# A shared first modulation: ten blocks on the tensor engine in 128-column passes, six on VectorE, none on GpSimd

## The chip, the cores and the metric

The kernel runs on one core of a Trainium2 chip. The metric is the device time of one execution in microseconds. The engines are called as the profile calls them: PE (TensorE, matrix products; its weight loads are listed apart as PEld), DVE (VectorE), ACT (ScalarE), POOL (GpSimd), and SP (SyncE, which issues the fetches).

## The reference

A trunk of two layers works on 512 latent and 256 context tokens of width 1024. Each layer first makes six vectors of 1024 numbers (a shift, a scale and a gate for each of its two halves) from a condition vector, once for the latent tokens (`c`) and once for the context (`c_ctx`). Then it normalises the tokens, scales and shifts them, and projects them. Only this beginning of layer 0 is touched by the change:

```python
silu_c = jax.nn.silu(c)
silu_cc = jax.nn.silu(c_ctx)
for l in range(DEPTH):                                   # 2 layers
    mod = silu_c @ w_mod[l] + b_mod[l]                   # (1024) @ (1024, 6144)
    mod_c = silu_cc @ w_mod[l] + b_mod[l]
    sh1, sc1, g1, sh2, sc2, g2 = jnp.split(mod[:, None, :], 6, axis=-1)
    csh1, csc1, cg1, csh2, csc2, cg2 = jnp.split(mod_c, 6)
    h = rms_norm(x, norm1[l]) * (1 + sc1) + sh1          # 512 latent tokens
    hc = rms_norm(ctx, norm1[l]) * (1 + csc1) + csh1     # 256 context tokens
    ... = jnp.split(h @ w_in[l], IN_SPLITS, axis=-1)     # and hc @ w_in[l]
    ...  # neighbourhood and grouped-query attention, gated merge, residual, SwiGLU FFN
```

All arithmetic is in float32.

## The kernel before

**Layout.** Tokens lie along the free dimension, latent tokens in columns 0 to 511 and context tokens in 512 to 767. Channels lie along the 128 partitions, so the width of 1024 is eight channel blocks `k`. Each large product is made of three float32r passes: a number is split in a high part (`h`, `wh`, copied on ACT) and the rest (`hl`, `wl`, a subtraction), and high by high, high by rest and rest by high are added in PSUM. A weight block is 128x1024 (512 KB).

**The front.** `Trunk.start` is the first stage. It fetches the eight token blocks (`x`, 384 KB each, latent and context together), squares and adds them up (`square`, L573; `total`, L576), takes the means on PE (`means`, L581), adds epsilon (`eps`, L586), takes the power -1/2 on POOL (`power`, L591), spreads the result over the partitions on PE (`widen`, L597), and multiplies each token block by it (`normed`, L603).

Meanwhile it makes the first sixteen of the layer's 48 modulation blocks, of 128 channels each: blocks 0 to 7 are the shifts of the channel blocks 0 to 7, and 8 to 15 their scales. Channel block `k` so needs modulation blocks `k` and `k + 8`. A block is made in one of three ways:

- `p`: on PE (`product`, L611), with the weight block as the loaded operand and the two condition columns (latent and context) as a moving operand of 2 columns, over eight steps; the result stands in PSUM (`mp`);
- `d`: on DVE, two reductions (`reduced`, L616) of the transposed weight block with a condition row spread over the partitions (`crow`), one for each condition;
- `g`: one reduction on DVE for the latent condition, and for the context condition a product on POOL (`times`, L620) that ACT adds up along the row (`summed`, L623).

`settle` (L628 and L631) adds the bias on DVE, and for a scale also multiplies by the norm's gain. When a channel block has its shift and its scale, `modulate` scales and shifts it in place, on ACT (L638) or DVE (L640), once for the latent and once for the context columns. `high` copies the high part on ACT (L644), `low` subtracts on POOL or DVE (L648).

At last `multiply` (L673) does the first three projection blocks (`gk0`, `gv0`, `gq0`): for the 512 latent columns three passes for each channel block and projection block, and after all of these the same for the 256 context columns. Their weights are split by `whigh` (ACT, L659) and `wlow` (POOL or DVE, L663). Two rules of the plan fix their order: channel blocks `k` in rising order within a projection block, and the context columns of a projection block behind its latent ones.

**The order.** The string `FIRST` gives the order of the fetches and how each modulation block is made (`x` is a token block, `w` a projection weight). `HOWU`, `HOWL` and `HOWW` name the engine of `modulate`, `low` and `wlow` for each block (a is ACT, v DVE, g POOL). From these `start` makes a list of operations, each with an engine, a cost, what it waits for, and an urgency. `Ops.run` is a list planner: it gives each engine a clock, takes the operation that can begin first (at a tie, the more urgent one), and writes the instructions in the order of these planned beginnings. That order is then fixed for each engine. Fetches are planned, and issued by SP, in the order of `FIRST`. A fetch of a modulation block waits until an earlier block of the same buffers has been used up, which the plan writes as `free[-5]`. Where PE has a gap in the plan, `run` fills it to 80% with small products of the identity (`idle`, L725, 0.215 us each in the plan).

The planned costs that matter here are `PROD` for a product on PE, 1.14 us for a reduction, and those of `low` (0.87 on DVE, 1.76 on POOL) and `wlow` (1.13 and 2.31).

**What follows.** Behind the front stand the rest of layer 0's projections and its attention, in an order written from a plan of their own, then the merge, the output projection and the FFN, and layer 1. The remaining modulation blocks are made beside these on DVE. The front's small pool has five row buffers of 128x1024 (two for `crow`, three `junk`) and five weight buffers; the tiles `x`, squares, `h` and `hl` come from a common store of 45 slots of 128x768.

Of the kernel before, what the change touches and what calls it, by code (L numbers as in the profile page):

```python
# [13 lines left out]
F32R = mybir.dt.float32r  # L14
AF = mybir.ActivationFunctionType
ALU = mybir.AluOpType
# [4 lines left out]
P = 128  # L21
D = 1024
KB = D // P
# [21 lines left out]
for _n in ORDER:  # L45
    for _j in range(COLS[_n][1]):
# [28 lines left out]
]  # L75


FIRST = "x x x x 10p x x x x 0g 8d 1g 13p w 9p w 2p 11g 12p 3d w 4g 5g 6g 14d 7d 15g"

HOWU, HOWL, HOWW = "aaavaaav", "ggvggvgv", "ggv"  # L80
START, HOP, LAND = 4.06, 0.15, 0.25
SAME = dict(v=0.22, a=0.0, g=0.0, p=0.0)
WARM = 0.8
PROD = 2.5


RATE = dict(a=(0.06, 0.00083, "a"), e=(0.28, 0.00083, "a"), v=(0.065, 0.00105, "v"), w=(0.065, 0.00058, "v"),
            g=(0.07, 0.00218, "g"), p=(0.0, 0.19, "g"))
# [175 lines left out]
class Ops:  # L264
# [6 lines left out]
    def add(self, engine, cost, run, args, after, urgency):  # L271
        self.ops.append((engine, cost, run, args, after, urgency))
        return len(self.ops) - 1
# [51 lines left out]
class Trunk:  # L325
# [208 lines left out]
    def start(self, h, pool, others):  # L534


        nc, d = self.nc, self.d
        mod = self.mod[0]
        spans = ((0, S), (S, T))
        nt = T // P  # L540
        row = lambda n, count: [pool.tile([P, D], F32, tag="row", name=self.name(n)) for _ in range(count)]
        crow, junk = row("crow", 2), row("junk", 3)

        more = pool.tile([P, 16], F32, tag="more", name=self.name("more"))
        nc.vector.tensor_copy(more[:, 0:8], self.bmod[:, 0, 0:8])
        nc.vector.tensor_scalar(more[:, 8:16], self.bmod[:, 0, 8:16], 1.0, None, op0=ALU.add)
        tiles, x, sqs, rb, raws = {}, [], [], {}, {}
        todo = Ops()
        add = todo.add

# [12 lines left out]
        rows = []  # L563
# [41 lines left out]
        def fetch(n, src):  # L605
            raws[n] = self.raw(src, pool=pool)

        def product(n, i):
            m = self.bank(tiles, i)[:, 2 * n : 2 * n + 2]
            for j in range(KB):  # L610
                nc.tensor.matmul(  # L611
                    m, raws[n][:, j * P : (j + 1) * P], self.ccol[:, 2 * j : 2 * j + 2],
                    start=(j == 0), stop=(j == KB - 1), skip_group_check=True)

        def reduced(n, s):
            nc.vector.tensor_tensor_reduce(  # L616
                junk[0], raws[n], crow[s], 1.0, 0.0, ALU.mult, ALU.add, mod[:, s, n : n + 1])

        def times(n, to):
            nc.gpsimd.tensor_tensor(to, raws[n], crow[1], op=ALU.mult)  # L620

        def summed(n, to):
            nc.scalar.activation(to, to, AF.Copy, accum_out=mod[:, 1, n : n + 1])  # L623

        def settle(n, i):
            m = mod[:, :, n] if i is None else self.bank(tiles, i)[:, 2 * n : 2 * n + 2]
            if n < KB:
                nc.vector.tensor_scalar(mod[:, :, n], m, more[:, n : n + 1], None, op0=ALU.add)  # L628
            else:
                k = n - KB  # L630
                nc.vector.tensor_scalar(  # L631
                    self.A[0][0][:, :, k], m, more[:, n : n + 1], self.norms[:, 0, k : k + 1], op0=ALU.add, op1=ALU.mult)
# [7 lines left out]
                nc.vector.tensor_scalar(u, u, scale, shift, op0=ALU.mult, op1=ALU.add)  # L640

        def high(k):
            h[0].append(self.slot("h", F32R))
            nc.scalar.activation(h[0][k], x[k], AF.Copy)  # L644

        def low(k, eng):
            h[1].append(self.slot("hl", F32R))
            (nc.gpsimd if eng == "g" else nc.vector).tensor_tensor(  # L648
                h[1][k], x[k], h[0][k][:].bitcast(F32), op=ALU.subtract)

# [24 lines left out]
        def evac(i):  # L675
            reach(others[i])

        loaded, got, free, wdone, sums = [], {}, [], [], []
        products = 0
        last = None  # L680
        for what in FIRST.split():
            if what == "x":
                k = len(loaded)
                loaded.append(add("d", 1.09, token, (k,), [], 1))
                sq = add("a", 0.74, square, (k,), [loaded[k]], 1)
                last = add("v", 0.87, total, (k,), [last, sq], 1) if k else sq
                if k < KB - 1:
                    continue
                last = add("v", 0.08, eps, (), [add("p", 1.28, means, (), [last], 0)], 0)
                early = [  # L690
                    add("p", c, widen, (s,), [add("g", g, power, (s,), [last], 0)], 0)
                    for s, c, g in ((0, 0.86, 0.96), (1, 0.43, 0.63))]
                ready = [
                    [add("v", c, normed, (k, s), [early[s], loaded[k]], 2) for s, c in ((0, 0.6), (1, 0.33))]
                    for k in range(KB)]
            elif what == "w":
                i = len(wdone)
                hi = add("a", 0.95, whigh, (i,), [add("d", 1.45, wraw, (i,), [], 1)], 3)
                eng = HOWW[i]
                wdone.append((hi, add(eng, 2.31 if eng == "g" else 1.13, wlow, (i, eng), [hi], 3)))  # L700
            else:
                n, how = int(what[:-1]), what[-1]
                src = d["wmod0"][products] if how == "p" else d["wmodT"][n]
                at = add("d", 1.45, fetch, (n, src), free[-5] if len(free) >= 5 else [], 1)
                which = None
                if how == "p":
                    which = products
                    products += 1
                    users = ends = [add("p", PROD, product, (n, which), [at], 3)]
                else:  # L710
                    users = [add("v", 1.14, reduced, (n, s), [at] + rows, 3) for s in range(1 + (how == "d"))]
                    ends = users
                    if how == "g":
                        to = junk[1 + len(sums) % 2]
                        users = users + [add("g", 2.31, times, (n, to), [at] + rows + sums[-2:-1], 3)]
                        sums.append(add("a", 1.04, summed, (n, to), users[-1:], 3))
                        ends = ends + sums[-1:]
                free.append(users)
                got[n] = add("v", 0.16, settle, (n, which), ends, 1)
        for t, n in ((self.cos, "cos"), (self.sin, "sin")):  # L720
# [7 lines left out]
        for k in range(KB):  # L728
            eng = HOWU[k]
            us = [add(eng, c, modulate, (k, s, eng), [ready[k][s], got[k], got[k + KB]], 2)  # L730
                  for s, c in (((0, 0.7), (1, 0.5)) if eng == "a" else ((0, 0.46), (1, 0.33)))]
            hi = add("a", 0.74, high, (k,), us, 2)
            halves.append([hi, add(HOWL[k], 1.76 if HOWL[k] == "g" else 0.87, low, (k, HOWL[k]), [hi], 2)])
# [1057 lines left out]
    def run(self):  # L1791
        nc, tc, d = self.nc, self.tc, self.d
        joint = [(0, S), (S, T)]
        self.flow = None
        with (
# [9 lines left out]
            h = ([], [])  # L1805
            with (
                tc.tile_pool(name="ps0n", bufs=1, space=PSUM, reuse_waits="tile") as psn,
                tc.tile_pool(name="ps0", bufs=1, space=PSUM, reuse_waits="tile") as psa,
                tc.tile_pool(name="n0", bufs=1, reuse_waits="tile") as pool_,
            ):  # L1810
                self.psum = dict(n=psn, a=psa)
                pool = _Bufs(pool_, dict(rs=1, row=5, more=1, wr=5), dict(qt=self.spool))
                self.constants(cpool)
                at = Front()
                spare = _Bufs(None, {}, dict(qt=self.spool))
                todo = self.prologue(0, h, joint, spare, at)
                self.start(h, pool, todo)
            xd = [self.dpool.tile([P, S], F32, name=f"xd{k}") for k in range(KB)]
            for l in range(DEPTH):
# [3 lines left out]
                n = spans[-1][1]  # L1823
# [3 lines left out]
                with (  # L1827
# [7 lines left out]
                    if not last:  # L1835
                        crow, junk = self.conditions(stack.enter_context(
                            tc.tile_pool(name=f"c{l}", bufs=1, reuse_waits="tile")))
                        one = lambda l, n: lambda: self.mod_one(l, n, crow, junk)
                        beside = [one(0, n) for n in range(16, 44)]
                    with tc.tile_pool(name=f"m{l}", bufs=1, reuse_waits="tile") as pool_:  # L1840
                        pool = _Bufs(pool_, dict(rs=2, qt=5), slots)
# [4 lines left out]
                        x = []  # L1846
# [22 lines left out]
                    h = ([], [])  # L1869
                    with tc.tile_pool(name=f"f{l}", bufs=1, reuse_waits="tile") as pool_:  # L1870
                        own = dict(acc=2, sq=2, u=2, qt=4, we=4) if last else dict(ws=1, tt=TEMPS, ps=7)
                        pool = _Bufs(pool_, dict(own, rs=2), None if last else slots)
# [24 lines left out]
                    if not last:  # L1897
                        at = Front()
# [125 lines left out]
def _layout(a):  # L2024
# [6 lines left out]
    def blocks(m):  # L2031

        k, n = m.shape
        return m.reshape(k // P, P, n // P, P).transpose(2, 1, 0, 3).reshape(n // P, P, k)

    win = []
    for l in range(DEPTH):
# [17 lines left out]
        gain=np.concatenate([two(a["q_gain"]), two(a["k_gain"])]).T,  # L2055
        wmod0=blocks(wm[0][:, : 2 * D])[[int(w[:-1]) for w in FIRST.split() if w[-1] == "p"]],
        wmodT=wmt.reshape(DEPTH * 48, P, D),
# [25 lines left out]
```

## Time and profile before

| | us |
|---|---|
| three runs before | 2013.2, 2014.64, 2015.53 (median 2014.64) |
| the profiled execution | 2013.65 |
| its span, first to last instruction | 2011.8 |
| PE busy in the span | 1947.7 |
| DVE busy | 1382.1 |
| ACT busy | 889.5 |
| POOL busy | 450.0 |
| last matmul of `multiply` (front) begins | 84.43 |

The mean granted clock of PE over the span was 0.982 of full speed.

In a row of instruction groups stand the line, the engine, the operation, what it writes and reads with the shapes, the count, then the busy time in us and the mean of one in ns, then the idle time of that engine just before them and what ended it. A row in order of time begins with its start and its length in us; several instructions of one kind can be merged in a row, with their count behind an `x`. A matmul of float32 (not float32r) is recorded as two matmuls. The time of an instruction can overlap that of the next one on its engine.

### The profile page before, as it was taken

The page shows a single profiled execution, that of the slowest core. Times are in us where ns is not written, and L with a number is a line of the kernel's source. Part 1 is how long each engine was busy: PE and PEld are TensorE (multiplying, and loading weights), DVE is VectorE, ACT ScalarE, POOL GpSimd, SP SyncE. Part 2 cuts the span into 40 slices and gives each one's busy share as a digit, 9 for nine tenths or more (in the row PEclk, how much of TensorE's full clock was granted, in tenths as well). Part 3 has the DMA queues.
Part 4 walks back from the last instruction along what each step waited for, and adds up shares of the span by engine and source line. Part 5 has one row for each costly group of instructions (what it writes and reads, how often), then busy time and mean ns, then how long its engine had stood idle before and what let it go on. Part 6 is the DMA issues. An engine that isn't in the chain of part 4 may idle for free. (4 is left out here: it accounts for less than half of the span.)

```text
span 2011.8 us, 29695 instructions
## 1 busy us (share of the span) xinstructions
PE 1947.7 (97%) x11516; PEld 1767.4 (88%) x11516; DVE 1382.1 (69%) x2498; ACT 889.5 (44%) x1646; POOL 450.0 (22%) x236
## 2 busy tenths in 40 slices
PE   7999999999989999999999989999999999999998
PEld 7898999988889999889899878889988998888887
DVE  7577888779787998888857576888654563232326
ACT  4466666552235533333334345666553442222224
POOL 5522213213300000000000014332322003534444
PEclk7899999999999999999999989999999999999999
DMA  7211112234464244456422432112233532323233
GB/s 287 65 55 50 38 53 87 64 112 161 136 246 143 67 134 135 142 162 202 134 82 61 125 111 64 56 48 64 77 89 110 195 110 87 113 76 118 79 115 95
DMA packets 73405, 218.61 MB, mean 109 GB/s; under 512 B 8624, under 2 KB 10800, under 8 KB 73264
## 3 DMA queue, kind: packets, MB, share of 16 engines
q1 hardware_dynamic: 73264, 216.71, 34.2%
q8 instruction: 91, 1.49, 0.3%
q14 instruction: 50, 0.41, 0.1%
HBM read 204.62 MB, written 6.82 MB: 105 GB/s over the span
## 5 line engine op out<-in xcount | busy, mean ns | idle before, releaser
L361 POOL TENSOR_TENSOR wl<-wr,wh 128x1024 fp32r<-128x1024 f32 (+2 forms) x156 | 330.7, 2124 | 713.7 <-ACT wh L359 684.4
L359 ACT ACTIVATE wh<-wr 128x1024 fp32r<-128x1024 f32 (+2 forms) x257 | 235.5, 919 | 547.2 <-issue 197.1
L374 PE MATMUL pj<-h,wh 128*128 128x512 f32 (+1 forms) x720 | 262.5, 367 | 4.0 <-DVE mb L1437 1.5
L374 PE MATMUL pj<-hl,wh 128*128 128x512 f32 (+1 forms) x720 | 254.4, 354 | 3.1 <-DVE hl L530 3.1
L374 PE MATMUL pj<-h,wl 128*128 128x512 f32 (+1 forms) x720 | 254.2, 353 | 0.0
L374 PE MATMUL po<-ph,wh 128*128 128x512 f32 (+1 forms) x560 | 193.2, 347 | 0.0
L374 PE MATMUL po<-pl,wh 128*128 128x512 f32 (+1 forms) x560 | 192.8, 345 | 0.0
L374 PE MATMUL po<-ph,wl 128*128 128x512 f32 (+1 forms) x560 | 191.3, 345 | 0.0
L1580 PE MATMUL qu<-r,w 128*128 128x384 f32 x960 | 175.3, 335 | 1.8 <-ACT tt L1587 1.8
L1580 PEld LDWEIGHTS qu<-r,w 128*128 128x128 f32 x960 | 166.7, 188 | 4.0 <-ACT tt L1587 3.9
L1447 DVE SCALAR_TENSOR_TENSOR x<-po,G,x 128x256 f32<-128x256 f32 (+3 forms) x160 | 91.9, 588 | 113.3 <-PE po L374 113.0
L496 POOL TENSOR_TENSOR rs<-rs,expo 128x2 f32<-128x2 f32 (+2 forms) x8 | 6.2, 772 | 678.6 <-DVE rs L495 678.6
L374 PEld LDWEIGHTS pj<-h,wh 128*128 128x128 f32 x720 | 137.6, 191 | 19.3 <-DVE mb L1437 1.8
L374 PEld LDWEIGHTS pj<-hl,wh 128*128 128x128 f32 x720 | 137.7, 191 | 18.1 <-DVE hl L530 4.0
L374 PEld LDWEIGHTS pj<-h,wl 128*128 128x128 f32 x720 | 137.2, 191 | 18.6
L374 PE MATMUL pf<-h,wh 128*128 128x512 f32 (+1 forms) x400 | 146.8, 367 | 1.0 <-ACT h L529 1.0
L374 PE MATMUL pf<-hl,wh 128*128 128x512 f32 (+1 forms) x400 | 146.7, 367 | 1.1 <-DVE hl L530 0.9
L374 PE MATMUL pf<-h,wl 128*128 128x512 f32 (+1 forms) x400 | 146.3, 366 | 0.0
L1007 ACT ACTIVATE pth<-tp 128x512 fp32r<-128x512 f32 x176 | 103.5, 596 | 65.9 <-PE tp L1057 37.4
L1008 DVE TENSOR_TENSOR ptl<-tp,pth 128x512 fp32r<-128x512 f32 x176 | 119.8, 685 | 14.2 <-ACT pth L1007 12.5
L374 PEld LDWEIGHTS po<-ph,wh 128*128 128x128 f32 x560 | 105.7, 189 | 14.1 <-ACT wh L359 1.1
L374 PEld LDWEIGHTS po<-pl,wh 128*128 128x128 f32 x560 | 105.8, 189 | 13.0
(243 smaller groups left out, 4524.3 us busy)
## 6 DMA issues: line engine op xcount, KB each, us to landing
wr<-wmodT SPq DMA_DIRECT2D x91, 512.0 KB, 3.8
wr<-wfi SPq DMA_DIRECT2D x88, 512.0 KB, 3.6
wr<-win SPq DMA_DIRECT2D x68, 512.0 KB, 3.6
wr<-wo SPq DMA_DIRECT2D x32, 512.0 KB, 4.3
wr<-wfo SPq DMA_DIRECT2D x40, 384.0 KB, 3.1
wr<-wp SPq DMA_DIRECT2D x32, 256.0 KB, 2.6
wr<-wfo SPq DMA_DIRECT2D x32, 256.0 KB, 2.7
x<-x SPq DMA_DIRECT2D x16, 384.0 KB, 7.6
```

The lines of the kernel that those rows point to most:

```text
L359: nc.scalar.activation(hi, raw, AF.Copy)
L361: (eng or nc.gpsimd).tensor_tensor(lo, raw, hi[:].bitcast(F32), op=ALU.subtract)
L374: nc.tensor.matmul(ps[:, : b - a], u[:, c], v[k][:, a:b], start=(k == 0 and i == 0), stop=(k == nk - 1 and i == 2),)
L496: nc.gpsimd.tensor_tensor(r[:, :nb], r[:, :nb], self.expo[:, :nb], op=ALU.pow)
L1007: nc.scalar.activation(hi, tp, AF.Copy)
L1008: nc.vector.tensor_tensor(lo, tp, hi[:].bitcast(F32), op=ALU.subtract)
L1447: self.nc.vector.scalar_tensor_tensor(x[j][:, f:u], ps[:, f - a : u - a], self.G[l][i][:, s, j : j + 1], x[j][:, f:u], op0=ALU.mult, op1=A ...
L1580: nc.tensor.matmul(banks[bank], u[:, c], v, start=(first and k == 0 and i == 0), stop=(k == kn - 1 and i == 2), skip_group_check=True)
```

## The change

- `FIRST` is written anew. PE makes ten of the sixteen blocks (8 to 15, 6 and 7), DVE six (0 to 5), each with two reductions. No block is made in the way `g`; `times` and `summed` are gone.
- A product on PE now reads the two condition columns 64 times over, as a moving operand of 128 columns, and writes 128 columns of PSUM, of which the first two are used. The planned cost `PROD` goes from 2.5 to 1.8, that of a reduction from 1.14 to 1.2.
- All `low` and `wlow` are on DVE; POOL keeps only the two powers. One `modulate` stays on DVE, for channel block 7.
- The fetch order begins with a modulation block, and weight blocks are mixed in among the token blocks. Seven weight buffers take the place of five, one `junk` row that of three.
- The tiles for `h` and `hl` are taken from the store at the start and not when they are written.

```diff
-FIRST = "x x x x 10p x x x x 0g 8d 1g 13p w 9p w 2p 11g 12p 3d w 4g 5g 6g 14d 7d 15g"
+FIRST = "8p x x 0d x x 9p x x 1d x x w 10p 2d w 11p 3d w 12p 4d 13p 5d 14p 6p 15p 7p"
+AHEAD = 7
-HOWU, HOWL, HOWW = "aaavaaav", "ggvggvgv", "ggv"
+HOWU, HOWL, HOWW = "aaaaaaav", "vvvvvvvv", "vvv"
-PROD = 2.5
+PROD = 1.8
...
-        crow, junk = row("crow", 2), row("junk", 3)
+        crow, junk = row("crow", 2), row("junk", 1)
...
+        for k in range(KB):
+            h[0].append(self.slot("h", F32R))
+            h[1].append(self.slot("hl", F32R))
...
+        def moved(i):
+            return self.bank(tiles, i)[:, i // 2 % 4 * P : i // 2 % 4 * P + P]
+
         def product(n, i):
-            m = self.bank(tiles, i)[:, 2 * n : 2 * n + 2]
             for j in range(KB):
                 nc.tensor.matmul(
-                    m, raws[n][:, j * P : (j + 1) * P], self.ccol[:, 2 * j : 2 * j + 2],
+                    moved(i).rearrange("p (a b) -> p a b", b=2), raws[n][:, j * P : (j + 1) * P],
+                    self.ccol[:, 2 * j : 2 * j + 2].unsqueeze(1).to_broadcast([P, P // 2, 2]),
                     start=(j == 0), stop=(j == KB - 1), skip_group_check=True)
...
-        def times(n, to):
-            nc.gpsimd.tensor_tensor(to, raws[n], crow[1], op=ALU.mult)
-
-        def summed(n, to):
-            nc.scalar.activation(to, to, AF.Copy, accum_out=mod[:, 1, n : n + 1])
-
         def settle(n, i):
-            m = mod[:, :, n] if i is None else self.bank(tiles, i)[:, 2 * n : 2 * n + 2]
+            m = mod[:, :, n] if i is None else moved(i)[:, 0:2]
...
-                at = add("d", 1.45, fetch, (n, src), free[-5] if len(free) >= 5 else [], 1)
+                at = add("d", 1.45, fetch, (n, src), free[-AHEAD] if len(free) >= AHEAD else [], 1)
...
-                    users = [add("v", 1.14, reduced, (n, s), [at] + rows, 3) for s in range(1 + (how == "d"))]
-                    ends = users
-                    if how == "g":
-                        to = junk[1 + len(sums) % 2]
-                        users = users + [add("g", 2.31, times, (n, to), [at] + rows + sums[-2:-1], 3)]
-                        sums.append(add("a", 1.04, summed, (n, to), users[-1:], 3))
-                        ends = ends + sums[-1:]
+                    users = ends = [add("v", 1.2, reduced, (n, s), [at] + rows, 3) for s in range(2)]
...
-                pool = _Bufs(pool_, dict(rs=1, row=5, more=1, wr=5), dict(qt=self.spool))
+                pool = _Bufs(pool_, dict(rs=1, row=3, more=1, wr=AHEAD), dict(qt=self.spool))
```

More of the change, by code (lines that the diff above doesn't have):

```diff
@@ L642, in high @@
         def high(k):
-            h[0].append(self.slot("h", F32R))
             nc.scalar.activation(h[0][k], x[k], AF.Copy)
         def low(k, eng):
-            h[1].append(self.slot("hl", F32R))
             (nc.gpsimd if eng == "g" else nc.vector).tensor_tensor(
@@ L676, in evac @@
             reach(others[i])
-        loaded, got, free, wdone, sums = [], {}, [], [], []
+        loaded, got, free, wdone = [], {}, [], []
         products = 0
```

## The prediction

> **What bounds the kernel now.** I read the page's busy shares first, then the stretches of the first 85 us, then the instruction groups of VectorE and GpSimd in that part, and last the order of time around the places where they meet. In the table of stretches the columns are: stretch, length, busy time (instructions) of PE, its weight loads, DVE, ACT and POOL, granted PE clock, DMA share, GB/s.
>
> ```profile
> PE 1947.7 (97%) x11516; PEld 1767.4 (88%) x11516; DVE 1382.1 (69%) x2498; ACT 889.5 (44%) x1646; POOL 450.0 (22%) x236
> 20.00:72.70 52.70, 42.54 (x191) 36.57 (x191) 49.03 (x70) 25.03 (x37) 37.60 (x16) 0.71 0.53 189
> 32.00:36.00 4.00, 4.00 (x17) 3.71 (x18) 4.00 (x10) 3.00 (x5) 3.20 (x2) 0.50 0.92 329
> 36.00:40.00 4.00, 4.00 (x18) 3.81 (x19) 3.78 (x5) 2.36 (x3) 4.00 (x2) 0.50 1.03 421
> 56.00:60.00 4.00, 4.00 (x27) 3.58 (x26) 3.93 (x5) 2.16 (x5) 3.92 (x3) 1.00 0.15 56
> 72.70:84.70 12.00, 12.00 (x92) 11.26 (x90) 2.12 (x4) 5.83 (x11) 6.44 (x3) 1.00 0.07 16
> 84.70:2011.80 1927.10, 1878.44 (x11141) 1705.02 (x11139) 1320.91 (x2406) 848.48 (x1585) 402.89 (x214) 0.99 0.34 105
> ```
>
> ```profile
> 8.35 0.96 DVE L576 TENSOR_TENSOR sq<-sq,sq 128x768 f32<-128x768 f32 x1 [3.74 <-ACT sq L573]
> 71.72 0.96 DVE L648 TENSOR_TENSOR hl<-x,h 128x768 fp32r<-128x768 f32 x1 [0.91 <-ACT h L644]
> 84.43 0.28 PE L673 MATMUL pj<-h,wl 128*128 128x256 f32 x1
> ```
>
> PE is the bound over the whole (1947.7 of 2011.8 us), and after 84.7 it is busy 1878.44 of 1927.10 us. Whatever the front saves is therefore handed on to the end nearly one for one. Inside the front PE is not the bound: from 20 to 72.7 VectorE is busy 49.03 of 52.70 us. Its last piece of work, the low half `hl` of the eighth channel block, runs 71.72 to 72.68. From then on PE alone decides, 12.00 of 12.00 us, until the front's last matmul ends at 84.71. So the question is when VectorE finishes, and what PE has left then.
>
> VectorE's 49 us are not all work. These are its costly groups up to 72.7, the undisturbed weight split of the later kernel, and three places in order of time:
>
> ```profile
> L616 DVE CUSTOM_DVE_ANT_0 junk<-wr,crow 128x1024 f32<-128x1024 f32 x15 | 28.9, 1928 | 0.4 <-DMA wr<-wmodT 0.2
> L576 DVE TENSOR_TENSOR sq<-sq,sq 128x768 f32<-128x768 f32 x7 | 6.7, 957 | 6.4 <-ACT sq L573 6.2
> L603 DVE TENSOR_TENSOR x<-x,rb 128x512 f32<-128x512 f32 x8 | 5.5, 683 | 1.6 <-PE rb L597 1.6
> L648 DVE TENSOR_TENSOR hl<-x,h 128x768 fp32r<-128x768 f32 x3 | 5.1, 1688 | 0.9 <-ACT h L644 0.9
> L631 DVE TENSOR_SCALAR A<-mod,more,norms_sb 128x2 f32<-128x2 f32 x4 | 4.0, 1000 | 0.6 <-ACT junk L623 0.6
> L603 DVE TENSOR_TENSOR x<-x,rb 128x256 f32<-128x256 f32 x8 | 3.3, 418 | 0.2 <-PE rb L597 0.2
> L663 DVE TENSOR_TENSOR wl<-wr,wh 128x1024 fp32r<-128x1024 f32 x1 | 3.4, 3430 | 0.0
> L640 DVE TENSOR_SCALAR x<-x,A,mod 128x512 f32<-128x512 f32 x2 | 1.1, 542 | 0.0
> L640 DVE TENSOR_SCALAR x<-x,A,mod 128x256 f32<-128x256 f32 x2 | 0.8, 403 | 0.0
> L361 DVE TENSOR_TENSOR wl<-wr,wh 128x1024 fp32r<-128x1024 f32 x33 | 40.1, 1222 | 12.8 <-ACT wh L359 12.5
> L620 POOL TENSOR_TENSOR junk<-wr,crow 128x1024 f32<-128x1024 f32 x7 | 21.7, 3104 | 16.9 <-DMA wr<-wmodT 16.9
> ```
>
> ```profile
> 58.82 3.40 POOL L620 TENSOR_TENSOR junk<-wr,crow 128x1024 f32<-128x1024 f32 x1
> 59.98 3.33 DVE L616 CUSTOM_DVE_ANT_0 junk<-wr,crow 128x1024 f32<-128x1024 f32 x1
> 63.37 1.21 DVE L616 CUSTOM_DVE_ANT_0 junk<-wr,crow 128x1024 f32<-128x1024 f32 x1
> ```
>
> ```profile
> 22.56 2.94 POOL L591 TENSOR_TENSOR rs<-rs,expo 128x4 f32<-128x4 f32 x2 [2.52 <-DVE rs L586]
> 23.59 0.22 DVE L628 TENSOR_SCALAR mod<-mod,more 128x2 f32<-128x2 f32 x1
> 23.72 1.22 DVE L616 CUSTOM_DVE_ANT_0 junk<-wr,crow 128x1024 f32<-128x1024 f32 x1
> 24.86 0.28 DVE L631 TENSOR_SCALAR A<-mod,more,norms_sb 128x2 f32<-128x2 f32 x1
> ```
>
> The same reduction (L616, a 128x1024 product summed along the row) takes 1.21 us at 63.37, with GpSimd idle, and 3.33 us at 59.98, while GpSimd's product (L620) runs from 58.82 to 62.22. It ends 1.09 us after GpSimd's does, about its own length: it stood still and then ran. So GpSimd's large operations hold up VectorE's. The surplus, from the rows: reductions 28.9 - 15 x 1.22 = 10.6 us; low halves 5.1 - 3 x 0.96 = 2.2; the weight split 3.43 - 1.22 = 2.2; the four small `A` updates 4.0 - 4 x 0.28 = 2.9 (0.28 as the one at 24.86). Together 17.9 us.
>
> **The change part by part.**
>
> Removed: GpSimd's seven products (21.7 us), its five low halves and two weight splits, and with them the 17.9 us. I book all of it, as all three kinds of large GpSimd work go; only the two small powers remain. ScalarE's seven row sums go as well; they only matter through the waits that hung on them.
>
> Moved to VectorE: five more low halves, 5 x 0.96 = 4.8 us, and two weight splits, 2 x 1.22 = 2.4. Taken from it: twelve reductions in place of fifteen, 3 x 1.2 = 3.6 us less, and the modulation of one channel block, 0.54 + 0.40 = 0.9 us, which goes to ScalarE. ScalarE is busy 25.03 of the 52.70 us and loses seven row sums, so I book nothing there; the cover is VectorE's 49 us.
>
> VectorE now takes from its first running total at 8.35 to 72.68, 64.3 us. New: 64.3 - 17.9 + 4.8 + 2.4 - 3.6 - 0.9 = 49.1 us. Two corrections. It starts later: the fetch order puts a 512 KB block ahead of the first token block, and another between the second and third. At the 421 GB/s of the stretch 36 to 40 each is 1.25 us; with the ScalarE copies of the condition rows pressing in between I put the first total at 10.4, 2.1 us later. Against that, the new order lays reductions between the totals, where VectorE idled 6.4 us behind the squares. Adding up all that the new list gives VectorE, at the spacing of starts (they overlap: the update starting at 23.59 takes 0.22 but the next starts at 23.72, 0.13 later), gives 42.4 us: 7 totals at 0.88, 12 reductions at 1.22, 8 normalisations at 0.96, 16 updates at 0.13 or 0.19, one modulation at 0.8, 8 low halves at 0.88, 3 splits at 1.12, one epsilon. Walking the list in the planner's order with these prices leaves some 4.5 us of idle time, mostly behind the powers and their spreading, so the end falls at 10.4 + 42.4 + 4.5 = 57.3. The difference above, without the regained idle time, gives 8.35 + 2.1 + 49.1 = 59.6. I take 58.2.
>
> PE: ten products for five, each eight loads and passes of a 128x128 block, recorded as sixteen.
>
> ```profile
> 27.31 7.13 PE L611 MATMUL mp<-ccol_sb,wr 128*128 128x2 f32 x48
> 35.73 3.41 PE L611 MATMUL mp<-ccol_sb,wr 128*128 128x2 f32 x16
> 40.42 0.63 PE L673 MATMUL pj<-h,wh 128*128 128x512 f32 x1
> 40.85 0.63 PE L673 MATMUL pj<-hl,wh 128*128 128x512 f32 x1
> 54.78 2.96 PE L725 MATMUL idle<-ident_sb 128*128 128x128 f32 x25
> 75.07 0.39 PE L673 MATMUL pj<-h,wh 128*128 128x512 f32 x1
> 75.29 0.39 PE L673 MATMUL pj<-hl,wh 128*128 128x512 f32 x1
> 84.31 0.28 PE L673 MATMUL pj<-hl,wh 128*128 128x256 f32 x1
> ```
>
> No row shows a product with 128 columns. The nearest is the filler `idle` (L725): the same 128x128 f32 load and a 128-column pass, 2.96 us for 25 records at full clock, 0.118 each, so 16 x 0.118 = 1.9 us a product. The other end is the two-column product at half clock, 3.41 us for 16. I take 2.0, the filler's, because the stretches say what the clock does: from 32 to 36 PE worked all 4.00 us, on two-column products mostly (three run from 27.31 to 34.44, a fourth from 35.73), and was granted 0.50; from 56 to 60, after 38 and 25 filler records, it was granted 1.00. Wide passes hold the clock, narrow ones let it fall. The repeated reading of two columns as the moving operand (step zero) has no row either; I give it the filler's price, with the same far end.
>
> What PE has left when VectorE ends: in the planner's order channel block 5 comes last but one (its shift, by reduction, settles last) and block 7 last, and the matmuls stand in fixed order: from block 5 on, nine groups are left of three 512-column passes, 75.07 to 75.29 = 0.23 us apart (0.43 at half clock, 40.42 to 40.85), 27 x 0.23 = 6.2 us, and then all 72 passes of 256 columns, 0.12 apart (84.31 to 84.43), 8.6 us: 14.8 us. Block 5 is ready 0.9 us before block 7, at 57.3, and the front ends at 72.1. I add 1 us for handovers, as the same walk put the kernel before at 82.4 where it ended at 84.7, part of that by half clock after a stall that the new order does not have. **Front's end: 73.1 to 73.7 against 84.7, a gain of 11 us.**
>
> The longest kind of PE wait behind 85 us (total, times, longest), and the fetches of such blocks (count, size, us to landing):
>
> ```profile
> PE rb L499 <- POOL rs L496: 5.2, 3, 3.1
> wr<-wmodT SPq DMA_DIRECT2D x91, 512.0 KB, 3.8
> ```
>
> Fetches: as many blocks as before, seven buffers for five. The fifteenth (`15p`) waits for the reductions of block 3, near 43, and SP's queue holds `7p`, cosine, sine and the next weights behind it. It lands some 3.8 us later and is settled near 49; block 5's last reduction ends at 52, which hides it. With 3 us less cover it would be the last. The early allocation of `h` changes only which slots are used; one row buffer less twice and two more for blocks fill the same space. I cost these at nothing; if a later slot had to wait the price would be that of the waits past the front, some 2 us, as the largest there now reaches 3.1.
>
> Sum: the profiled execution took 2013.65 us (span 2011.8), 1.0 below the median of 2014.64. 2013.65 - 11 = 2002.65, so 2003.6 as a median.
>
> **The rivals.**
>
> ```profile
> L555 PE MATMUL cp<-ident_sb,ccol_sb 128*128 128x128 f32 x32 | 5.5, 351 | 3.5 <-DMA ident_sb<-ident 3.5
> ```
>
> (1) GpSimd's powers block as its products did. [...] The trace: two powers run from 22.56 to 25.50, and the reduction that starts at 23.72 beside them takes 1.22 us, its free price. If they did block, the pair of reductions that the new order sets beside the powers, 2 x 1.22, would follow them instead: 2.4 us more, 2006.0. [...] I give it 8%.
>
> (2) PE becomes the bound. If wide products ran at half clock, 3.4 us each, and the 512-column passes with them, PE's list would be 10 x 3.4 + 72 x 0.43 + 8.6 = 73.6 us, and the spreading of the condition at its start (5.5) makes 79.1. Begun at 3.5 it ends at 82.6 with no idle time and no filler; with the 49 fillers that the planner sets into its gaps, at two records of 0.213, 21 us, at 103.5. That is between 2012 and 2033, and I put 2020. It decides from the point where list, fillers and waits pass 81.2 us. At full clock they are 10 x 1.9 + 72 x 0.23 + 8.6 + 5.5 = 49.7 and 11.6 of fillers, 20 below. For it speaks that PE had 0.71 of its clock over 20 to 72.7; against it the filler rows. 6%.
>
> (3) Mixed: the products cost 2.6 us, with some stretches at half clock; updates that wait for PE stop VectorE, as they stand in its queue ahead of reductions. Ten times 0.6 is 6 us on PE, of which VectorE's queue takes over some 4 to 8: 2008 to 2011. 10%.
>
> (4) The gain is made and then lost past the front, in slots or fetches: anything from 2007 to 2015; the 48.7 us in which PE idles after 84.7 have no single large cause. 6%.
>
> **How the numbers follow.** The likeliest case, 70%, gives 2003.6, with its own range 2000 (a gain of 14.5: no handover cost and VectorE done at 55) to 2007.5. What can be told from no change here is about 0.2%, 4 us: 2010.6 is the border. Range: the likeliest with rivals 1 and 3, 2000 to 2011, leaves out rival 2, most of 4 and the tails. Faster: 0.70 + 0.08 + 0.08 + 0.01; same: 0.02 of rival 3 and 0.05 of rival 4; slower: rival 2. The case that VectorE is freed but nothing moves is in 4.
>
> **What the new profile would show.** Right: reductions (twelve) at 1.22 us and low halves at 0.96 throughout; last low half between 56 and 60; ten products at about 1.9 us with the clock at 1.00 from 30 on; front's last matmul at 72 to 75; and the stretch behind it as long as before, 1927 us. Wrong: products of 3 us or more or a clock of 0.5 between 35 and 60; VectorE waiting for PE ahead of updates for more than 6 us; or a stretch behind the front longer by some us.

## The result, and the profile after

The changed kernel took 2002.28 us as a median of four runs (1998.07 to 2005.09), the kernel before 2015.09 beside it. The ratio is 0.9935, with a 95% interval of 0.9912 to 0.9957. In a second measurement of five runs it took 1999.96 us, and the kernel before 2012.45 beside it, a ratio of 0.9937 (0.9921 to 0.9953). So the change saved 12.8 and 12.5 us. The forecast was 2003.6 us, a saving of 11, and faster. The profiled execution of the first measurement has a span of 2002.5 us and took 2004.31.

The rows that answer to those of the prediction follow, first the stretches, in the same columns as there:

```profile
PE 1943.7 (97%) x11598; PEld 1763.5 (88%) x11598; DVE 1363.6 (68%) x2497; ACT 884.2 (44%) x1634; POOL 414.6 (21%) x222
28.00:32.00 4.00, 4.00 (x39) 4.00 (x38) 4.00 (x11) 3.30 (x5) 0.00 (x0) 1.00 1.03 410
32.00:36.00 4.00, 4.00 (x38) 4.00 (x37) 4.00 (x11) 3.88 (x6) 0.00 (x0) 1.00 1.02 402
69.70:2002.50 1932.80, 1880.64 (x11141) 1704.41 (x11139) 1318.44 (x2406) 849.57 (x1585) 405.06 (x214) 0.99 0.34 105
```

The granted clock is 1.00 in these two stretches of 4 us, where it was 0.86 and 0.50. The order of time shows VectorE's last low halves, PE's last pass of the front, one product, and the reductions beside GpSimd's powers:

```profile
24.54 1.22 DVE L624 CUSTOM_DVE_ANT_0 junk<-wr,crow 128x1024 f32<-128x1024 f32 x1
24.70 2.88 POOL L595 TENSOR_TENSOR rs<-rs,expo 128x4 f32<-128x4 f32 x2 [24.26 <-DVE rs L590]
25.80 1.22 DVE L624 CUSTOM_DVE_ANT_0 junk<-wr,crow 128x1024 f32<-128x1024 f32 x1
...
28.18 1.95 PE L618 MATMUL mp<-ccol_sb,wr 128*128 128x128 f32 x16
...
53.86 1.83 DVE L648 TENSOR_TENSOR hl<-x,h 128x768 fp32r<-128x768 f32 x2 [1.48 <-ACT h L645]
...
69.43 0.28 PE L673 MATMUL pj<-h,wl 128*128 128x256 f32 x1
```

VectorE is done at 55.69 in place of 72.68, and the front ends at 69.71 in place of 84.71, 15.0 us earlier. Both reductions beside the powers take 1.22 us. The groups of VectorE's costly work now all have the price that they had before with GpSimd idle:

```profile
L624 DVE CUSTOM_DVE_ANT_0 junk<-wr,crow 128x1024 f32<-128x1024 f32 x12 | 14.6, 1219 | 0.1
L648 DVE TENSOR_TENSOR hl<-x,h 128x768 fp32r<-128x768 f32 x8 | 7.5, 953 | 1.5 <-ACT h L645 1.5
L663 DVE TENSOR_TENSOR wl<-wr,wh 128x1024 fp32r<-128x1024 f32 x3 | 3.7, 1220 | 0.0
```

The stretch behind the front took 1932.8 us, where it took 1927.1 before. So the front gave 15.0 us, the stretch behind it took back 5.7, and the profiled span shows 9.3.

### The profile page after: what moved, and what is told of

The parts are those of the page before. It is cut to its first block, busy times and chain, and to the rows that moved or that the text cites. A ratio compares the mean times of both kernels' runs of the same rounds, so it can differ in the third digit from the quotient of the medians.

```text
span 2002.5 us, 29811 instructions
## 1 busy us (share of the span) xinstructions
PE 1943.7 (97%) x11598; PEld 1763.5 (88%) x11598; DVE 1363.6 (68%) x2497; ACT 884.2 (44%) x1634; POOL 414.6 (21%) x222
```

## The experiments

"Front" is the end of the front's last matmul, "behind" the rest of the span. Both are from the one profile of each kernel; the total is the median. Each ratio is to the kernel before as it was measured beside that run: 2015.09 us for the changed kernel, 2013.43 for two columns, the halves back and the late slots, 2013.79 for GpSimd out alone, wide passes alone, nine products and the first run of the other list, 2012.45 for the four others. So compare rows by their ratios, not by their totals.

| kernel | last low half begins | front | behind | total | ratio to before (95%) |
|---|---|---|---|---|---|
| before | 71.7 | 84.7 | 1927.1 | 2015.09 | 1 |
| changed | 54.7 | 69.7 | 1932.8 | 2002.28 | 0.9935 (0.9912 to 0.9957) |
| changed, again | 55.4 | 70.4 | 1926.6 | 1999.96 | 0.9937 (0.9921 to 0.9953) |
| GpSimd out alone | 67.1 | 79.0 | 1927.2 | 2008.24 | 0.9974 (0.9963 to 0.9984) |
| wide passes alone | 71.7 | 83.9 | 1936.4 | 2017.86 | 1.0022 (1.0012 to 1.0032) |
| changed, two columns | 66.9 | 85.0 | 1924.6 | 2012.38 | 0.9996 (0.9986 to 1.0007) |
| changed, 32 columns | 59.2 | 74.6 | 1927.8 | 2004.89 | 0.9970 (0.9954 to 0.9985) |
| changed, no fillers | 60.1 | 75.0 | 1928.3 | 2004.44 | 0.9957 (0.9940 to 0.9974) |
| changed, GpSimd's halves back | 52.9 | 70.6 | 1928.6 | 2002.35 | 0.9952 (0.9936 to 0.9969) |
| changed, late slots | 55.1 | 70.1 | 1925.3 | 1998.72 | 0.9928 (0.9914 to 0.9943) |
| changed, nine products | 59.0 | 71.0 | 1926.1 | 2000.20 | 0.9931 (0.9913 to 0.9950) |
| another list | 52.2 | 64.3 | 1924.0 | 1991.48 | 0.9893 (0.9873 to 0.9914) |
| another list, again | 51.9 | 64.1 | 1921.1 | 1989.57 | 0.9883 (0.9865 to 0.9901) |

### GpSimd left out alone

```diff
 (on the kernel before)
-FIRST = "... 0g 8d 1g 13p w 9p w 2p 11g 12p 3d w 4g 5g 6g 14d 7d 15g"
+FIRST = "... 0d 8d 1d 13p w 9p w 2p 11d 12p 3d w 4d 5d 6d 14d 7d 15d"
-HOWU, HOWL, HOWW = "aaavaaav", "ggvggvgv", "ggv"
+HOWU, HOWL, HOWW = "aaavaaav", "vvvvvvvv", "vvv"
... (h and hl are kept by block number, not in the order of writing)
```

> The kernel before, with GpSimd left out alone: its seven product blocks get a second VectorE reduction each, its low halves and weight splits go to VectorE; five two-column products, fetch order and buffers stay. Theory A (two things set the front: GpSimd's hold on VectorE, and how much VectorE has to do): VectorE gets rid of 17.9 us of standing still but takes on 7 x 1.2 + 5 x 0.96 + 2 x 1.22 = 15.6 us, so its last low half ends near 67 to 71 and the front's last matmul near 79 to 83 (84.7 before, 69.7 with the whole change), total 2009 to 2014; reductions at 1.22 us throughout. Rival B (the standing still was all): the front ends at 70 to 72 and the total is that of the whole change, about 2002. Rival C (it stood on something else than GpSimd): reductions still take 2 to 3 us.

The front ended at 79.0, 5.7 us earlier, at the near end of theory A; the total, 2008.24, is 0.8 below its range. The reductions of this kernel, as a group with their count, busy time and mean:

```profile
L618 DVE CUSTOM_DVE_ANT_0 junk<-wr,crow 128x1024 f32<-128x1024 f32 x22 | 26.9, 1221 | 0.3
```

All 22 run at 1.22 us, where 15 had a mean of 1.93. So GpSimd was what VectorE stood still for, and rival C falls. But VectorE has 26.9 us of reductions now, where it had 28.9 with the stops in them. So rival B falls too: taking the stops away is worth only what is left when VectorE does GpSimd's work itself.

### Wide passes alone

```diff
 (on the kernel before)
-                    m, raws[n][...], self.ccol[:, 2 * j : 2 * j + 2],
+                    moved(i)..., raws[n][...], self.ccol[...].unsqueeze(1).to_broadcast([P, P // 2, 2]),
... (moved as in the change; settle reads its first two columns)
```

> The kernel before, with its five products in 128-column passes and nothing else changed. Theory A (VectorE sets the front there, held by GpSimd; PE's clock does not matter before VectorE is done): products take 1.95 us, the clock is higher between 24 and 44, but the last low half still ends at 71 to 73 and the front at 82 to 85; total within 3 us of the kernel before. Rival (the width alone makes the gain): front end below 76 and total below 2006.

The front ended at 83.9, 0.8 us earlier, and the last low half began at 71.7, as before: theory A. PE's clock, 1.00 from 36 to 40 where it was 0.50, was worth next to nothing while VectorE was late. In the same stretch of time PE now only waits longer (before, it was busy all 4.00 us of 36 to 40):

```profile
36.00:40.00 4.00, 1.64 (x6) 1.05 (x6) 3.96 (x5) 2.15 (x3) 4.00 (x2) 1.00 1.02 418
```

The total is 0.2% above the kernel before, and not below it: 4.1 us, where theory A had at most 3. In the profile the loss lies behind the front: the FFN of layer 0, from its first to its last matmul of the kinds `qu` and `qv`, took 451.8 us against 443.0, with 13.0 us of waits before these matmuls against 7.6. PE's instructions there are the same. This is one profile; why the median of its runs lies above the kernel before too is open.

### The change with two columns

```diff
 (on the changed kernel)
-                    moved(i).rearrange("p (a b) -> p a b", b=2), raws[n][:, j * P : (j + 1) * P],
-                    self.ccol[:, 2 * j : 2 * j + 2].unsqueeze(1).to_broadcast([P, P // 2, 2]),
+                    moved(i)[:, 0:2], raws[n][:, j * P : (j + 1) * P], self.ccol[:, 2 * j : 2 * j + 2],
```

> The whole change, but the ten products read the two condition columns once (two-column passes); everything else, order and fillers too, as in the changed kernel. Theory A (the granted clock follows the width of the passes, two columns do not count as work): the clock falls to 0.5 between 28 and 48, products take 2.4 to 3.4 us in place of 1.95, and the front's last matmul ends at 73 to 90, most likely 80: total 2006 to 2020. [...]

The whole gain is gone: front 85.0, ratio 0.9996 (0.9986 to 1.0007). Stretches (in the same columns as above), products, and one row of fillers, in order of time:

```profile
28.00:32.00 4.00, 4.00 (x21) 4.00 (x20) 2.34 (x7) 1.42 (x3) 0.00 (x0) 0.50 1.03 410
32.00:36.00 4.00, 4.00 (x20) 4.00 (x20) 2.74 (x7) 3.96 (x6) 0.00 (x0) 0.50 1.03 407
48.00:52.00 4.00, 4.00 (x20) 4.00 (x20) 2.70 (x5) 0.21 (x1) 0.00 (x0) 0.50 0.17 68
...
9.18 1.84 PE L618 MATMUL mp<-ccol_sb,wr 128*128 128x2 f32 x16
30.37 3.41 PE L618 MATMUL mp<-ccol_sb,wr 128*128 128x2 f32 x16
33.64 4.19 PE L718 MATMUL idle<-ident_sb 128*128 128x128 f32 x18
45.61 6.82 PE L618 MATMUL mp<-ccol_sb,wr 128*128 128x2 f32 x32
```

PE is busy 4.00 of 4.00 us and has half its clock. A product then takes 3.41 us, where one at 9.18, between wide passes and at a clock of 1.00, takes 1.84, and the wide one 1.95. So the narrow product is not dear by itself; the lower clock, 0.50 here where several stand close together, is. That clock also held for what stood next: the 18 filler records from 33.64, of 128 columns, take 4.19 us, and 2.17 in the changed kernel. VectorE pays for it, since it waits for products whose results its updates read. This group idled 0.5 us behind PE in the changed kernel:

```profile
L632 DVE TENSOR_SCALAR A<-mp,more,norms_sb 128x2 f32<-128x2 f32 x8 | 2.2, 280 | 9.2 <-PE mp L618 9.2
```

The last low half begins 12.2 us later than in the changed kernel, and PE takes 18.1 us from there in place of 15.0.

Idle gaps do not explain the fall to 0.50 here: between the first product and the fall PE's gaps are 1.44 and 0.95 us, and the changed kernel has the like of both (1.56 and 1.06) and keeps 1.00.

### 32 columns

```diff
 (on the changed kernel)
-                    ... .to_broadcast([P, P // 2, 2]),
+                    moved(i)[:, 0:32]..., ... .to_broadcast([P, 16, 2]),
```

> The changed kernel with the two condition columns read 16 times over, 32 columns a pass, in place of 128. With two columns the front ended at 85.0, with 128 at 69.7, and the loads take the same time. Theory A (the clock follows how much of the time the array streams columns, and 32 of 128 is too little): front end at 78 to 85, clock 0.5 to 0.7 from 24 to 52, total 2006 to 2013. Rival (any more than a few columns will do): front end within 1 us of 69.7 and the total of the changed kernel. I lean to A, 60 to 40.

Neither: the front ended at 74.6, in between. The clock was half from 24 to 36, where products, spreading and fillers stand, 0.78 from 36 to 40, and full from 40 on, where 512-column passes stand between the products:

```profile
32.00:36.00 4.00, 4.00 (x20) 4.00 (x20) 2.87 (x7) 3.94 (x6) 0.00 (x0) 0.50 1.03 407
44.00:48.00 4.00, 4.00 (x32) 3.78 (x32) 4.00 (x8) 0.00 (x0) 0.00 (x0) 1.00 0.83 319
```

So products of 32 columns did not keep the clock in the first of these mixtures, and did in the second. That the mixture over some us counts is argued from this, not shown by a run of its own; widths between 32 and 128 were not tried.

### No fillers

```diff
 (on the changed kernel)
-WARM = 0.8
+WARM = 0.0
```

> The changed kernel without the small identity products that fill PE's gaps in the front; the order of all other instructions stays. Theory A (PE needs work in the gaps, else the clock falls): PE stands idle from 10.5 to 14.2 and from 16 to 23, the granted clock is 0.5 for the second to fourth products and the spreads, and the front ends at 71 to 76, most likely 73; total 2 to 5 us above the changed kernel. Rival (ten wide products hold the clock by themselves): front end within 1 us of 69.7.

Theory A: front 75.0, total 4.5 us above the changed kernel as measured beside it (1999.96). The long gap is 6.65 us; behind it even the wide product is at half clock (3.76 us, of which a part overlaps the next row):

```profile
24.17 2.72 PE L585 MATMUL st<-ones,sq 128*128 128x1 f32 x12 [6.65 <-DVE sq L580]
26.75 3.76 PE L618 MATMUL mp<-ccol_sb,wr 128*128 128x128 f32 x16
32.31 5.52 PE L618 MATMUL mp<-ccol_sb,wr 128*128 128x128 f32 x48
```

The last row is three products at 1.84 each, at full clock again. The granted clock was 0.83 from 12 to 16 and 0.50 from 24 to 28, where the changed kernel had 1.00 in both. So it fell here where PE had stood idle, 3.02 us ahead of the second product (3.34 us) and 6.65 us ahead of the means. In the kernel with two columns it fell to 0.50 with narrow passes close together and no gap above 1.44 us.

### GpSimd's halves back

```diff
 (on the changed kernel)
-HOWU, HOWL, HOWW = "aaaaaaav", "vvvvvvvv", "vvv"
+HOWU, HOWL, HOWW = "aaaaaaav", "ggvggvgv", "ggv"
```

> The whole change, but five low halves and two weight splits are back on GpSimd, as in the kernel before. Theory A (any large GpSimd operation with VectorE's two-input operations makes one stand still while the other runs, and VectorE gives up 5 x 0.96 + 2 x 1.22 = 7.2 us of work for 14 us of GpSimd's): the stops eat most of what VectorE gives up, the last low half comes within 2 us of the changed kernel's 55.7, the front ends at 70 to 73, total 2001 to 2006, some reductions at 2 to 3.4 us. Rival (VectorE's load alone counts): the front ends 4 to 7 us earlier, 63 to 66. Rival (the hold is as dear as it was before): the front ends past 76.

Theory A, at its near end: front 70.6, last low half begun at 52.9. One meeting cost 1.5 us:

```profile
43.05 1.84 POOL L648 TENSOR_TENSOR hl<-x,h 128x768 fp32r<-128x768 f32 x1 [7.85 <-ACT h L645]
43.28 2.69 DVE L624 CUSTOM_DVE_ANT_0 junk<-wr,crow 128x1024 f32<-128x1024 f32 x1
...
51.87 0.50 PE L673 MATMUL pj<-hl,wh 128*128 128x512 f32 x1 [1.25 <-POOL hl L648]
```

The reduction ends 1.08 us after the GpSimd operation, the same picture as in the kernel before. But with GpSimd's products gone there are few such meetings: all twelve reductions took 16.5 us, against 14.6. The last low half began 1.8 us earlier than in the changed kernel, and still the front did not end earlier: PE waited 1.25 us for a low half on GpSimd (last row). Leaving the halves on GpSimd so costs at most 0.9 us in the front. With the rest of the change in place, GpSimd's seven products are the part of its work that mattered.

### Nine products

```diff
 (on the changed kernel)
-... 14p 6p 15p 7p
+... 14p 6d 15p 7p
```

> The changed kernel with modulation block 6 moved from PE to VectorE (nine products, seven blocks by reduction). It asks which engine bounds the changed front: its PE rows stand end to end from 36.4 to 69.7. Theory A (PE bounds it from 36 on): 1.8 us of PE's work less, and the front ends at 68 to 69, unless the last low half comes so late that PE waits. Rival (VectorE bounds it): 2.4 us more on VectorE, last low half at 57.5 to 59 in place of 55.7, front end at 71 to 73. Walking the list with the measured prices gives 71.5 against 70.4 for the changed kernel, so I lean to the rival. Total within 2 us of the changed kernel either way.

The sizes are the rival's: last low half begun at 59.0, front 71.0 in place of 69.7 and 70.4. But that does not show that VectorE alone bounds the changed front, since theory A left out just this case, a last low half so late that PE waits. In the changed kernel the two engines meet. The profile shows no wait of PE for another engine between 28 and 69.7, and the low half of block 5, done at 54.82, is read by PE at 55.00, behind four fillers:

```profile
53.86 0.96 DVE L648 TENSOR_TENSOR hl<-x,h 128x768 fp32r<-128x768 f32 x1 [1.48 <-ACT h L645]
54.32 0.60 PE L719 MATMUL idle<-ident_sb 128*128 128x128 f32 x4
55.00 0.40 PE L673 MATMUL pj<-hl,wh 128*128 128x512 f32 x1
```

So more work on VectorE makes PE wait, as with the nine products (PE's weight loads waited 1.5 us in all for five low halves), and a VectorE that was done earlier would gain little here unless PE's list became shorter too.

### Late slots, and the changed kernel again

```diff
 (on the changed kernel: h and hl from the store where they are written)
+            h[0][k] = self.slot("h", F32R)
             nc.scalar.activation(h[0][k], x[k], AF.Copy)
...
+            h[1][k] = self.slot("hl", F32R)
```

> The whole change, but the tiles for h and hl are taken from the store when they are written, as in the kernel before, not at the start. It asks where 5.8 of the front's 15.1 us went in the profiled run of the changed kernel (the stretch behind the front took 1932.9 us against 1927.1). Theory A (the stretch behind the front varies by some us from one execution to the next, by half-clock spells and waits in the FFN): front end within 1 us of 69.6, the stretch behind it 1926 to 1934, total 1998 to 2005. Rival (other slots make later instructions wait): the stretch behind the front comes back to 1927 within 1 us and the total is 3 to 6 us below the changed kernel's, 1996 to 1999.

> The changed kernel itself once more, for a second profile and a narrower ratio. Theory A (the stretch behind the front varies from one execution to the next, mostly in the FFN of layer 0 and by short half-clock spells): front end within 0.5 us of 69.7, the stretch behind it somewhere in 1924 to 1934, not 1932.8 again; median total 1998 to 2003. Rival (the changed front makes the stretch behind it 5.8 us longer): 1932 to 1934 again, median 2002 to 2004.

With late slots the stretch behind was 1925.3, just below theory A's 1926 to 1934, which alone would speak for the rival. But the two-column kernel has the early slots and 1924.6, and the changed kernel itself, in a second profile, 1926.6. Of thirteen profiles with one order of instructions behind the front, that stretch took 1921 to 1936 us. So the 5.7 us were that execution's. By the ratios (0.9928 with late slots, 0.9935 and 0.9937 with early ones, their intervals overlapping) early slots could still cost 1 to 2 us.

The second profile's front ended at 70.4 and not within 0.5 us of 69.7, because even with 128-column passes the clock was not full throughout: 0.69 from 24 to 28 and 0.89 from 28 to 32. The spreading, for which VectorE's norms wait, took 2.74 us there and 1.66 in the first profile.

In the first profile of the changed kernel, a half-clock spell in layer 0's attention (0.50 from 178 to 180 us) and waits in its FFN make 4.4 of the 5.7 us: the attention took 1.6 us longer, the FFN 445.8 against 443.0. The first two rows are the same instructions before and after; the last two are the main waits of PE in the FFN after (total, times, longest), which were 1.8 and 5.8 before:

```profile
174.40:285.70 111.30, 110.72 (x752) 101.23 (x751) 93.38 (x185) 72.24 (x144) 26.05 (x14) 1.00 0.16 49
159.40:272.30 112.90, 112.31 (x752) 102.56 (x751) 93.61 (x185) 72.40 (x144) 26.18 (x14) 0.98 0.16 49
PE qu L1574 <- ACT tt L1581: 5.2, 4, 2.0
PE qv L1574 <- DVE tt L1954: 4.7, 4, 2.2
```

The 1.6 us go with a clock of 0.98 in place of 1.00. What sets off such a spell is not shown, and 1.3 of the 5.7 us are not placed.

### Another list

```diff
 (on the changed kernel)
-FIRST = "8p x x 0d x x 9p x x 1d x x w 10p 2d w 11p 3d w 12p 4d 13p 5d 14p 6p 15p 7p"
+FIRST = "x x x x x x x 10p x 1p 9d 6d 0p w 7p 8p 5p w 3p 2p 11p 4d 13p 12p w 14d 15d"
-HOWU, HOWL, HOWW = "aaaaaaav", "vvvvvvvv", "vvv"
+HOWU, HOWL, HOWW = "aaaaaaaa", "vvvvvvvv", "vvv"
```

> The changed kernel with another list: FIRST = x x x x x x x 10p x 1p 9d 6d 0p w 7p 8p 5p w 3p 2p 11p 4d 13p 12p w 14d 15d (eleven products, five blocks by reduction, the token blocks ahead), and all modulations on ScalarE. Theory A (the front's end is set by VectorE's list and by PE's 33 us of products and passes behind it, so that earlier norms and a scale and shift that come in pairs shorten it): walking the list with the measured prices puts the last low half at 52 and the front's end at 62.9; total 1990 to 1999, front end 62 to 65. Rival (fetches bound it, the same bytes at 410 GB/s to about 46 us): no earlier than 68, total as the changed kernel.

> The other list (eleven products, five blocks by reduction, token blocks ahead, all modulations on ScalarE) once more, beside the changed kernel in the same call. Theory A: front end 64.3 again, 5.4 us ahead of the changed kernel's, total 5 to 9 us below it, 1990 to 1996. Rival (its lead in the first measurement was a lucky stretch behind the front): total within 3 us of the changed kernel's.

Theory A: front 64.3 and 64.1, total 1991.48 and, beside the changed kernel's 1999.96, 1989.57. It beats both kernels. The token blocks come first, so the norms are ready while blocks still arrive; the reductions fall from twelve to ten; and the products stand in the part where the changed kernel had fillers (98 records there, 46 here). Which of the three gives how much was not tried:

```profile
L624 DVE CUSTOM_DVE_ANT_0 junk<-wr,crow 128x1024 f32<-128x1024 f32 x10 | 12.2, 1219 | 0.2 <-DMA wr<-wmodT 0.2
L618 PE MATMUL mp<-ccol_sb,wr 128*128 128x128 f32 x176 | 20.5, 274 | 1.6 <-DMA wr<-wmod 1.6
```

## Why the prediction was right, point by point

- **VectorE sets the front's end, and what it saves is handed on.** Right for the kernel before. In the changed kernel PE shows no wait for another engine after 28 us either, so the two engines bound the front together; the forecast had PE waiting for VectorE. In all kernels the front ends 12 to 18 us after the last low half begins. What a kernel gains in the median follows what its front gains to within 5 us, the wide passes alone being the furthest off. I had not priced that variation: the first profile gave back 5.7 of 15.0 us, the second nothing.
- **GpSimd's hold, 17.9 us.** Right in kind and in size as a surplus: reductions fell from 1.93 to 1.22, low halves to 0.95. As the main term it is misleading alone. With GpSimd's work put on VectorE and none moved to PE, it is worth 5.7 us in the front.
- **VectorE done at 58.2.** Mis-sized: 55.69. It began at 10.43 (10.4 forecast) and had 42 us of work as added up; idle time was some 3 us and not 4.5, and I had put 0.9 us on top towards the larger figure of 59.6, which kept the old idle time behind the squares.
- **Products at 2.0 us, clock kept by wide passes.** Right: 1.95, clock 1.00 in the first profile, with one spell of 0.69 in the second. Width alone did not keep it: without the fillers wide products took 3.34 and 3.76 us, with PE idle for 3.02 us ahead of the first and for 6.65 ahead of the means before the second. This is the step on which all hangs: with two columns it costs 15.3 us in the front and the whole gain. I gave it 6% to fail outright and 10% in part, and wrote of it as one price among others.
- **14.8 us of PE work behind block 5.** Right: its low half ends at 54.8, the front at 69.7. The 1 us for handovers was not there. With the 2.5 us above this is why the front came at 69.7 and not at 73.1 to 73.7.
- **Fetches and slots at nothing.** Not contradicted; early slots could cost 1 to 2 us by the ratios above. The row of waits by which I would have priced a late slot is not the longest kind, as I called it: in the kernel before PE waits 5.8 us in all for DVE ahead of `qv`, and one wait reaches 3.3. The sum does not use it.
- **Rivals.** The powers do not block: the two take 2.88 us, and both reductions beside them 1.22 each. PE did not become the bound in rival 2's way, by half its clock.
- **The signs named in advance.** The last low half (54.7, forecast 56 to 60) and the last matmul (69.4, forecast 72 to 75) came earlier than the signs of being right had them. A stretch behind the front longer by some us, named as a sign of being wrong, showed in the first profile (1932.8) and not in the second (1926.6).

The front gained 15.0 us where 11 was booked, 4.0 more, and the first profile gave 5.7 back behind it; that the first median came within 1.3 us of the forecast is in part these two against each other, and so in part luck. The second median lies 3.6 us below the forecast, but the kernel before was 2.2 us faster beside it too (2012.45 against 2014.64). The saving is the fairer measure: 12.8 and 12.5 us, forecast 11, with fronts that gained 15.0 and 14.3 in the two profiles. Why about 2 us of the front's gain is missing from both medians is open.

## What to carry to other kernels

Count a product on PE with few moving columns not by its own row but by the clock that it leaves to what follows: with two columns it cost 1.84 us among wide passes and 3.41 close to others of its kind, at a clock of 0.50, and with 128 columns 1.95. Parts of a change that share one bound can be worth little apart and much together: GpSimd left out alone gave 5.7 us in this front, wide passes alone 0.8, everything but the wide passes nothing (85.0), and the whole 15.0. So walk the engines' queues with the measured prices before ranking them. What the new order of fetches and the two more buffers are worth by themselves was not tried. Judge a change in a short front by that front's end in the trace; behind it 1930 us of the same instructions varied by 15 us.

## What the runs showed of the hardware that I had not expected

PE was granted half its clock while it was busy 4.00 of 4.00 us, with nothing but two-column products from 48 to 52 us. In the run with 32 columns the clock was 0.50 from 28 to 36, with spreading and fillers among the products, and 1.00 from 44 to 48, with 512-column passes among them. Two GpSimd powers on 128x4 and 128x2 took 2.88 us and held up neither of two VectorE reductions, while a GpSimd low half of 1.84 us made one take 2.69.
